# Output tiles that use two pools of accumulator banks in turn, and a small product that is placed later

## The chip, the core and the metric

The kernel runs on one core of a Trainium2 chip. A core has TensorE (PE, matrix products into PSUM, which has eight banks here), VectorE (DVE), ScalarE (ACT), GpSimd (POOL) and SyncE (SP, which issues the DMAs). Each engine works through its own instructions in order; between engines they wait on semaphores. The metric is the device time of one execution in microseconds, as the median of several runs.

## The reference

Two layers of a decoder trunk on x of shape (1, 512, 1024) in float32. Each layer is network 1, a token mixer, network 2, each behind an adaptive norm and added to x through a gate:

```python
mod = jax.nn.silu(c) @ w_mod[l] + b_mod[l]
sh1, sc1, g1, sh2, sc2, g2, sh3, sc3, g3 = jnp.split(mod[:, None, :], N_MOD, axis=-1)
h = _rmsnorm(x) * (1.0 + sc1) + sh1
x = x + HALF_STEP * g1 * _swiglu(h, ffn1_w_gate[l], ffn1_w_up[l], ffn1_w_down[l])
h = _rmsnorm(x) * (1.0 + sc2) + sh2
x = x + g2 * _hybrid_mixer(h, w_in[l], w_out[l], ...)
h = _rmsnorm(x) * (1.0 + sc3) + sh3
x = x + HALF_STEP * g3 * _swiglu(h, ffn2_w_gate[l], ffn2_w_up[l], ffn2_w_down[l])
```

`_swiglu` is (silu(h Wgate) * (h Wup)) Wdown, with 2816 hidden columns. The mixer joins stick-breaking attention, dilated attention and a gated recurrence, and projects back with w_out. The modulation `mod` is a product of one row with a 1024 x 9216 matrix for each layer.

## The kernel before, in words

Everything is kept transposed: x lives in SBUF as eight tiles X[0..7] (printed as x_84 to x_91), each 128 of the 1024 model columns by 512 tokens. Each float32 operand of a large product is split into a high and a low part (hi, lo), and a product is three matmuls (`triple`): hi*hi, hi*lo, lo*hi.

**Networks.** There are four (two in each layer). The 22 blocks of hidden columns are taken in three groups of 8, 8 and 6. In a group the gate and up products come first (PSUM tiles `m` and `a`; some pairs of blocks use a seven-product scheme, `seven`), then the down products: eight output tiles d = 0 to 7, each summed over the group's 8 (or 6) hidden blocks, so 24 (or 18) matmuls to a tile. The first two tiles of a group are made by `down_two` (it walks both tiles over the first n-2 blocks and then over the last two), the others by `down`. Each finished output tile is added to X[d] by one DVE instruction, `residual`, which multiplies by the gate and thereby empties the bank. In the last group of three of the four networks, tiles 2 to 7 are made in two halves of 256 tokens, so that the next norm (`norm`) can begin on the first half; then `first` starts the next stage's products with two `m` and two `a` banks.

**Banks.** PSUM is shared by two pools: `M` ("m", two banks) and `B` ("a", six banks). A tile is taken by `get`, which hands out the bank that is free the longest by the planner's account. In the kernel before, every output tile of a network takes an `m` bank.

**The modulation.** `background` runs through w_mod in pieces of 128 rows: DVE multiplies each piece by its value of silu(c) and adds it to `acc`; after eight pieces DVE reduces `acc` to 32 columns (`p`, an instruction that transposes and sums), PE sums over partitions with one small product (`a<-p,quads`), and DVE writes the result into `mod`. 16 such products are spread over the program.

**The order of the work.** The kernel is written as many generators ("streams"), which hand out steps. A planner (`Flow`, lines 229 to 356) runs them against its own account of when each engine and tile is ready, and always advances the step that can start first, with a bias by rank; what it emits is the fixed order of each engine's instructions. `Flow.start` (line 326) adds a margin to PE steps: MARGIN (0.65 us) for streams of rank 0, and LATE (line 66) for rank 4, which only `background` has. LATE is how long after its `p` the planner thinks ready it will place the small product at the earliest. Nearly all instructions are recorded by one helper, so the profile gives them line 116 (L116); tiles tell them apart.

Of the kernel before, what the change touches and what calls it, by code (L numbers as in the profile page):

```python
# [62 lines left out]
BR = -0.15  # L63
BA = (-0.1, -0.1)
BN = (-0.15, -0.1)
LATE = 2.0
LOP = ((1, 2, 3), (1, 2, 3, 4, 5, 6, 7))

SPANS = tuple((sum(GROUPS[:i]), n) for i, n in enumerate(GROUPS))
# [159 lines left out]
class Flow:  # L229
# [96 lines left out]
    def start(self, s):  # L326
# [6 lines left out]
        t = self.clk[st.engine] if st.engine != "SP" else self.clk["PE"]  # L333
        late = self.MARGIN if st.engine == "PE" and s[0] == 0 else LATE if st.engine == "PE" and s[0] == 4 else 0.0
        for a in st.deps:
# [24 lines left out]
def trunk(ctx, tc, x, c, w_mod, b_mod, f1g, f1u, f1d, w_in, w_out, qng, kng, hng, lbl, f2g, f2u, f2d, cf, out):  # L360
# [6 lines left out]
    def space(name, bufs, **kw):  # L367
        return ctx.enter_context(tc.tile_pool(name=name, bufs=bufs, **kw))
# [8 lines left out]
    M = Pool(F, space("psm", 2, space=PS), "m", [P, S], 2)  # L377
    B = Pool(F, space("psa", 6, space=PS), "a", [P, S], 6)
# [36 lines left out]
    def when(*keys):  # L415
        return lambda: all(k in done for k in keys)
# [526 lines left out]
    def part(w, k, i=None):  # L943

        o = slice(0, 256) if i is None else slice(i * P, (i + 1) * P)
        return tuple(z[:, k % 4, o] for z in w[k // 4])

    def triple(ps, wh, wl, xh, xl, start, stop, skip=False):
        T.matmul(ps, wh, xh, start=start, stop=False, skip_group_check=skip)
        T.matmul(ps, wh, xl, start=False, stop=False, skip_group_check=skip)  # L950
        T.matmul(ps, wl, xh, start=False, stop=stop, skip_group_check=skip)
# [184 lines left out]
    def residual(phase, d, ps, l, jg, cs):  # L1136
        if jg != 5 or not isinstance(phase, tuple):
            yield when(("mod", l, jg))
        yield Step("DVE", ps, bias=BR)
        V.scalar_tensor_tensor(X[d][:, cs], ps[:, cs], mod(l, jg, d), X[d][:, cs], ALU.mult, ALU.add)  # L1140
        drop(ps)
        for t in range(2):
            if cs.start <= t * HALF and cs.stop >= (t + 1) * HALF:
                done.add((phase, d, t))
# [32 lines left out]
    def ffn(phase, l, jsh, hs, last):  # L1177
# [3 lines left out]
        for f0, n in SPANS:  # L1181
# [58 lines left out]
            for f in range(f0, f0 + n, 2):  # L1240
# [15 lines left out]
                if f in fast:  # L1256
                    yield when((phase, "sums"))
                    for name, pools, fin in (("g", (M, M, B), gate_seven), ("u", (B, B, B), up_seven)):
                        w = yield from next_weight()
                        yield Step("PE", need=tuple((p, pools.count(p)) for p in (M, B) if p in pools))  # L1260
                        banks = [p.get() for p in pools]
# [6 lines left out]
                for pool, fin in ((M, gate_out), (B, up_out)):  # L1268
                    w = yield from next_weight()
                    for i in range(2):  # L1270
                        yield Step("PE", need=((pool, 1),))
                        ps = pool.get()
# [17 lines left out]

            def down(w, d, cs):
                yield when(keys[0])
                yield Step("PE", need=((M, 1),))
                ps = M.get()
                for k in range(n):
                    yield when(keys[k])
                    hi, lo = hid[k]
                    wh, wl = part(w, k, d % 2)
                    yield Step("PE", lo, wh, wl)
                    triple(ps[:, cs], wh, wl, hi[:, cs], lo[:, cs], k == 0, k == n - 1)  # L1300
                F.spawn(residual(key, d, ps, l, jg, cs), 0)

            def down_two(w, cuts):

                yield Step("PE", need=((M, 2),))
                banks = [M.get() for _ in range(2)]
                for ks in cuts:
                    for d, ps in enumerate(banks):
                        for k in ks:
                            yield when(keys[k])  # L1310
                            hi, lo = hid[k]
                            wh, wl = part(w, k, d)
                            yield Step("PE", lo, wh, wl)
                            triple(ps, wh, wl, hi, lo, k == 0, k == n - 1)
                        if ks[-1] == n - 1:
                            F.spawn(residual(key, d, ps, l, jg, FULL), 0)
# [4 lines left out]
            for d in range(0, whole, 2):  # L1321
                w = yield from next_weight()
                if d == 0:
                    yield from down_two(w, (range(n - 2), range(n - 2, n)))
                else:
                    for i in range(2):
                        yield from down(w, d + i, FULL)
                release(w)
            if whole < ND:
                ws = []  # L1330
                for t, cs in enumerate(HALVES):
                    for d in range(whole, ND):
                        if t == 0 and d % 2 == 0:
                            ws.append((yield from next_weight()))
                        w = ws[(d - whole) // 2]
                        yield from down(w, d, cs)
                        if t and d % 2:
                            release(w)
                WS.most -= MORE
# [649 lines left out]
```

## Time and profile before

| | |
|---|---|
| median of 3 runs | 2092.57 us (2092.12 to 2093.74) |
| the profiled execution's own time | 2094.81 us |
| its span, first to last instruction | 2092.4 us |
| PE busy in the span | 2050.3 us |
| DVE / ACT / POOL busy | 1586.0 / 1005.1 / 183.6 us |
| mean granted TensorE clock | 0.992 |
| matmul records | 12956 |

A row of the timeline has the start in us from the span's start, the time to the end of the last of the merged instructions, the engine, the line, the operation, the tiles (out<-in), the shape, the count, and in brackets the engine's idle time before it with what ended it. A matmul's recorded duration overlaps that of the next one, so merged rows overlap a little, and an idle gap of PE is counted from the end of the last matmul's record. Waits are listed as engine and tile, waited for engine and tile, total us, times, longest. Windows give each engine's busy time in a stretch of the span with its count of instructions, and the granted TensorE clock as a share of full speed.

### The profile page before, as it was taken

How to read it: one execution, taken by the hardware profiler on the slowest of the kernel's cores; microseconds unless marked ns; L12 is line 12 of the kernel's file. 1: busy time of each engine (PE TensorE's matmuls, PEld its weight loads, DVE VectorE, ACT ScalarE, POOL GpSimd, SP SyncE). 2: the span in 40 equal slices, each digit the busy share in tenths (PEclk: the TensorE clock that was granted, in tenths of full speed). 3: DMA queues.
4: the chain of work that ended last, by engine and by line, in shares of the span. 5: the costliest groups of instructions: out<-in, count | busy, mean ns of one | idle time of the engine just before them, and what ended most of it. 6: DMA issues, size and time to landing. Idle time of an engine off the chain costs nothing.

```text
span 2092.4 us, 32600 instructions
## 1 busy us (share of the span) xinstructions
PE 2050.3 (98%) x12956; PEld 1855.7 (89%) x12956; DVE 1586.0 (76%) x2510; ACT 1005.1 (48%) x1675; POOL 183.6 (9%) x224
## 2 busy tenths in 40 slices
PE   7999999999999999999999999999999999999999
PEld 6888889988888987999898899989888889889897
DVE  6887877686698776879686888867867978658584
ACT  5523434555855542544354253436476645325351
POOL 0000000150150100000010000012304200000000
PEclk8999999999999999999999999999999999999999
DMA  9376466211203245345524635643112141533321
GB/s 330 117 230 191 151 218 204 81 60 41 71 21 99 94 133 169 109 154 182 181 69 134 221 101 181 197 146 102 41 41 66 36 127 55 186 96 101 101 82 41
DMA packets 210569, 259.46 MB, mean 124 GB/s; under 512 B 8896, under 2 KB 192084, under 8 KB 210416
## 3 DMA queue, kind: packets, MB, share of 16 engines
q1 hardware_dynamic: 210160, 257.30, 38.5%
q8 instruction: 101, 1.65, 0.3%
q14 instruction: 52, 0.43, 0.1%
q0 software_dynamic: 256, 0.08, 0.0%
HBM read 255.25 MB, written 2.10 MB: 123 GB/s over the span
## 4 chain that ended last, share of the span: by engine, by line
PE 93%; DVE 4%; ACT 2%; issue 1%; DMA 1%; SPq 0%; DVEq 0%; ACTq 0%
PE m L116 56%; PE a L116 37%; ACT u L116 1%; DVE u L116 1%; DVE wt L116 1%; DVE x L116 1%; DVE h L116 1%; DVE acc L116 0%; ACT wt L116 0%; DMA w<-in_ffn_w_up_dram 0%; DMA u<-in_x_dram 0%; DVE k L116 0%; ACT L1471 0%; ACT L116 0%; SPq L116 0%
## 5 line engine op out<-in xcount | busy, mean ns | idle before, releaser
L116 ACT CAST wt<-w 128x1024 fp32r<-128x1024 f32 (+1 forms) x456 | 437.6, 975 | 328.4 <-PE m L116 124.0
L116 DVE TENSOR_TENSOR wt<-w,wt 128x1024 fp32r<-128x1024 f32 (+1 forms) x456 | 518.6, 1144 | 95.3 <-ACT wt L116 86.2
L116 PE MATMUL m<-u,wt 128*128 128x512 f32 (+1 forms) x2820 | 576.7, 362 | 6.3 <-DVE x L116 4.2
L116 PE MATMUL m<-h,wt 128*128 128x256 f32 (+1 forms) x2892 | 551.8, 342 | 11.6 <-ACT h L116 5.5
L116 PEld LDWEIGHTS m<-u,wt 128*128 128x128 f32 x2820 | 475.4, 190 | 85.7 <-DVE x L116 5.6
L116 PEld LDWEIGHTS m<-h,wt 128*128 128x128 f32 x2892 | 451.0, 192 | 69.4 <-ACT u L116 6.6
L116 PE MATMUL a<-h,wt 128*128 128x256 f32 (+1 forms) x2124 | 347.4, 318 | 0.0
L116 PEld LDWEIGHTS a<-h,wt 128*128 128x128 f32 x2124 | 308.3, 191 | 26.5
L116 DVE TENSOR_TENSOR u<-u 128x256 f32<-128x256 f32 (+4 forms) x444 | 255.3, 593 | 34.5 <-ACT u L116 30.7
L116 PE MATMUL a<-hs,wt 128*128 128x256 f32 x1944 | 250.8, 283 | 0.0
L116 POOL TENSOR_TENSOR u<-u 128x256 f32<-128x256 f32 x162 | 137.6, 869 | 1284.8 <-ACT u L116 1237.5
L116 PEld LDWEIGHTS a<-hs,wt 128*128 128x128 f32 x1944 | 241.0, 192 | 0.0
L116 DVE SCALAR_TENSOR_TENSOR x<-m,mod,x 128x512 f32<-128x512 f32 (+1 forms) x142 | 92.2, 651 | 111.7 <-PE m L116 111.0
L116 ACT ACTIVATE u<-u 128x512 f32<-128x512 f32 (+2 forms) x272 | 146.7, 567 | 49.2 <-POOL u L116 29.3
L116 DVE TENSOR_TENSOR w<-w 128x512 f32<-128x512 f32 x216 | 149.0, 690 | 6.2 <-DMA w<-in_ffn_w_gate_dram 0.6
L116 DVE SCALAR_TENSOR_TENSOR acc<-w,sc_c,acc 128x1024 f32<-128x1024 f32 x112 | 143.6, 1282 | 1.8
L116 PEld LDWEIGHTS a<-u 128*128 128x128 f32 x864 | 114.7, 191 | 11.8 <-issue 2.1
L116 ACT COPY u<-a 128x256 f32<-128x256 f32 (+1 forms) x149 | 58.1, 390 | 129.9 <-PE a L116 127.6
L116 PE MATMUL a<-u 128*128 128x64 f32 (+4 forms) x864 | 117.0, 282 | 1.9 <-DVE u L116 0.8
L116 ACT COPY u<-m 128x256 f32<-128x256 f32 (+1 forms) x119 | 49.7, 418 | 123.4 <-PE m L116 117.2
L116 ACT CAST u<-u 128x512 fp32r<-128x512 f32 (+1 forms) x96 | 58.4, 611 | 102.7 <-DVE u L116 93.4
L116 PE MATMUL m<-wt,h 128*128 128x256 f32 x768 | 99.7, 287 | 0.9 <-DVE u L116 0.9
(146 smaller groups left out, 1452.6 us busy)
## 6 DMA issues: line engine op xcount, KB each, us to landing
w<-in_w_mod_dram SPq DMA_DIRECT2D x128, 512.0 KB, 4.3
w<-in_ffn_w_gate_dram SPq DMA_DIRECT2D x88, 512.0 KB, 4.7
w<-in_ffn_w_up_dram SPq DMA_DIRECT2D x88, 512.0 KB, 4.9
w<-in_ffn_w_down_dram SPq DMA_DIRECT2D x80, 512.0 KB, 4.7
w<-in_w_in_dram SPq DMA_DIRECT2D x56, 512.0 KB, 3.8
u<-in_w_mod_dram SPq DMA_DIRECT2D x32, 256.0 KB, 6.0
w<-in_w_out_dram SPq DMA_DIRECT2D x24, 256.0 KB, 3.1
w<-in_ffn_w_down_dram SPq DMA_DIRECT2D x16, 256.0 KB, 5.7
```

The lines of the kernel that those rows point to most:

```text
L116: ins = fn(*args, **kw)
```

## The change

Two things change. The output tiles of a network take an `m` bank for even d and an `a` bank for odd d, in `down` and in `down_two`. And LATE grows from 2.0 to 5.0. No instruction is added or removed.

```diff
-LATE = 2.0
+LATE = 5.0
...
             def down(w, d, cs):
                 yield when(keys[0])
-                yield Step("PE", need=((M, 1),))
-                ps = M.get()
+                pool = (M, B)[d % 2]
+                yield Step("PE", need=((pool, 1),))
+                ps = pool.get()
...
             def down_two(w, cuts):
 
-                yield Step("PE", need=((M, 2),))
-                banks = [M.get() for _ in range(2)]
+                yield Step("PE", need=((M, 1), (B, 1)))
+                banks = [M.get(), B.get()]
```

Since the planner decides the order, the diff does not show what moves. Set beside each other, the two programs have PE's 12534 matmuls other than the 16 small products in the same order (only the norm's product over `ones` comes six matmuls later at three places); what differs there is the bank and where the small products stand. SP's and POOL's orders are the same; DVE's and ACT's are changed locally.

The first place is PE in network 2 of the first layer, the output tiles of the first group of hidden blocks (24 matmuls to a tile, the first two interleaved as 18, 18, 6, 6). Before:

```order
L116 MATMUL m<-u,wt 128x512 x42
L116 MATMUL a<-p,quads 128x32
L116 MATMUL m<-u,wt 128x512 x150
```

and now:

```order
L116 MATMUL m<-u,wt 128x512 x18
L116 MATMUL a<-u,wt 128x512 x18
L116 MATMUL m<-u,wt 128x512 x6
L116 MATMUL a<-u,wt 128x512 x6
L116 MATMUL m<-u,wt 128x512 x9
L116 MATMUL a<-p,quads 128x32
L116 MATMUL m<-u,wt 128x512 x15
L116 MATMUL a<-u,wt 128x512 x24
```

The tiles alternate between the pools, and the small product stands behind 57 of the matmuls instead of 42.

The second place is DVE at the same spot, from the small product's `p` on. Before:

```order
L116 TENSOR_REDUCE p<-acc 128x32
L116 SCALAR_TENSOR_TENSOR mod_92<-a,bcol_94 32x8 x4
L116 SCALAR_TENSOR_TENSOR x_84<-m,mod_92,x_84 128x512
L116 TENSOR_TENSOR wt<-w,wt 128x1024
L116 SCALAR_TENSOR_TENSOR x_85<-m,mod_92,x_85 128x512
```

and now:

```order
L116 TENSOR_REDUCE p<-acc 128x32
L116 TENSOR_TENSOR wt<-w,wt 128x1024 x2
L116 SCALAR_TENSOR_TENSOR mod_92<-a,bcol_94 32x8 x4
L116 SCALAR_TENSOR_TENSOR x_84<-m,mod_92,x_84 128x512
L116 SCALAR_TENSOR_TENSOR x_85<-a,mod_92,x_85 128x512
L116 SCALAR_TENSOR_TENSOR x_86<-m,mod_92,x_86 128x512
```

Two weight parts (`wt`, the low half of a weight) come ahead of the four instructions that read the small product; the additions to X (x_84 is tile 0) that empty the first banks come behind them.

The third place is PE where network 1 of the first layer ends and the mixer begins: the last group, two whole tiles, then tiles 2 to 7 in two halves, then the first products of the next stage from `h`. Before:

```order
L116 MATMUL m<-u,wt 128x512 x36
L116 MATMUL m<-u,wt 128x256 x129
L116 MATMUL a<-u,ones 128x256
L116 MATMUL m<-u,wt 128x256 x87
L116 MATMUL m<-h,wt 128x256 x24
L116 MATMUL a<-u,ones 128x256
L116 MATMUL m<-h,wt 128x256 x24
```

and now, from the end of the first product over `ones` on:

```order
L116 MATMUL a<-u,ones 128x256
L116 MATMUL a<-u,wt 128x256 x15
L116 MATMUL m<-u,wt 128x256 x18
L116 MATMUL a<-u,wt 128x256 x18
L116 MATMUL m<-u,wt 128x256 x18
L116 MATMUL a<-u,wt 128x256 x18
L116 MATMUL m<-h,wt 128x256 x30
L116 MATMUL a<-u,ones 128x256
L116 MATMUL m<-h,wt 128x256 x18
```

The last tile before the next stage (d = 7) is now in an `a` bank, and the one before it (d = 6) in an `m` bank, while the next stage starts with both `m` banks.

## Prediction

> **What bounds the kernel now.** I read the page's busy times first, then PE's waits, then the timeline of PE at each wait, then what DVE does there.
>
> ```profile
> PE 2050.3 (98%) x12956; PEld 1855.7 (89%) x12956; DVE 1586.0 (76%) x2510; ACT 1005.1 (48%) x1675; POOL 183.6 (9%) x224
> PE 93%; DVE 4%; ACT 2%; issue 1%; DMA 1%; SPq 0%; DVEq 0%; ACTq 0%
> ```
>
> PE is busy for 98% of the span and makes 93% of the chain that ended last. The change leaves PE's work as it is, so it can only win or lose in PE's waits and in the speed at which PE runs behind them. The waits of PE:
>
> ```profile
> PE m L116 <- DVE x L116: 7.5, 10, 2.0
> PE a L116 <- ACT u L116: 6.3, 10, 1.2
> PE m L116 <- ACT h L116: 5.5, 6, 1.7
> PE m L116 <- ACT u L116: 4.9, 6, 1.7
> PE a L116 <- DMA ident<-in_constants_dram: 3.2, 1, 3.2
> PE a L116 <- DVE p L116: 2.8, 1, 2.8
> ```
>
> The first row is PE waiting for an `m` bank that DVE has not emptied into X; the last is the small product waiting for its `p`. These are what the change can touch: 7.5 + 2.8 = 10.3 us, not all of it, but with what follows on each wait. No row names `wt`: PE never waits for a weight.
>
> For the price of a wait the undisturbed step is needed:
>
> ```profile
> L116 PE MATMUL m<-u,wt 128*128 128x512 f32 x2004 | 474.0, 394 | 3.8 <-DVE x L116 3.7
> L116 PE MATMUL m<-h,wt 128*128 128x256 f32 x1452 | 196.3, 288 | 9.5 <-ACT h L116 3.7 <-DVE x L116 3.3 <-ACT u L116 2.4
> 1815.68 10.14 PE L116 MATMUL m<-u,wt 128*128 128x512 f32 x44
> 688.27 3.04 PE L116 MATMUL m<-u,wt 128*128 128x256 f32 x24
> ```
>
> A 512-wide matmul is recorded with 0.394 us, and 44 of them take 10.14, so one follows the other after (10.14 - 0.394)/43 = 0.227. For 256 wide it is (3.04 - 0.288)/23 = 0.120. The rest of a record (0.167 in both cases) overlaps the next, so a gap of g in a row costs PE g + 0.17.
>
> **Part 1: the small product that waits** (network 2 of the first layer, first group's output tiles; PE, then DVE):
>
> ```profile
> 790.47 9.68 PE L116 MATMUL m<-u,wt 128*128 128x512 f32 x42
> 802.98 0.64 PE L116 MATMUL a<-p,quads 128*128 128x32 f32 x2 [2.83 <-DVE p L116]
> 803.43 8.77 PE L116 MATMUL m<-u,wt 128*128 128x512 f32 x26
> 801.68 1.25 DVE L116 TRANSPOSE_TENSOR_REDUCE p<-acc 128x32 f32<-128x1024 f32 x1
> ```
>
> Behind the gap the 26 matmuls take 8.77 where 0.394 + 25 x 0.227 = 6.07 is normal: 2.70 more. The cause is the granted clock, which stands at half in these windows:
>
> ```profile
> 798.00:802.00 4.00, 2.16 (x10) 1.46 (x8) 3.93 (x5) 0.53 (x1) 0.00 (x0) 1.00 0.60 185
> 802.00:805.00 3.00, 2.02 (x6) 1.73 (x7) 2.19 (x6) 0.00 (x0) 0.00 (x0) 0.52 0.95 313
> 1829.00:1832.00 3.00, 3.00 (x9) 2.37 (x9) 1.52 (x2) 0.03 (x1) 0.00 (x0) 0.59 1.10 349
> 1162.00:1170.00 8.00, 6.56 (x30) 5.46 (x31) 5.96 (x10) 2.40 (x3) 0.00 (x0) 1.00 0.65 197
> ```
>
> The small product itself also runs slow, 0.45 to the next start where the one at 1825.66 below has 0.14: 0.31. The site costs 2.83 + 0.17 + 0.31 + 2.70 = 6.0 us. In the changed order it stands behind 57 matmuls instead of 42. PE gets there at 790.47 + 57 x 0.227 = 803.4; `p` is done at 801.68 + 1.25 = 802.9, and the DVE instructions ahead of it are the same. So the wait goes, by a margin of only 0.5 us.
>
> **Part 2: output tiles that wait for a bank.** Tile 0 of a group ends after 42 matmuls and tile 2 begins after 48. With two `m` banks tile 2 needs the bank of tile 0, so DVE has 6 x 0.227 = 1.4 us to empty it. Twice it is late:
>
> ```profile
> 1150.90 11.04 PE L116 MATMUL m<-u,wt 128*128 128x512 f32 x48
> 1163.44 5.07 PE L116 MATMUL m<-u,wt 128*128 128x512 f32 x21 [1.50 <-DVE x L116]
> 1162.64 0.75 DVE L116 SCALAR_TENSOR_TENSOR x<-m,mod,x 128x512 f32<-128x512 f32 x1
> 1825.66 0.31 PE L116 MATMUL a<-p,quads 128*128 128x32 f32 x2
> 1825.80 0.94 PE L116 MATMUL m<-u,wt 128*128 128x512 f32 x3
> 1828.79 7.59 PE L116 MATMUL m<-u,wt 128*128 128x512 f32 x25 [2.04 <-DVE x L116]
> 1827.98 1.41 DVE L116 SCALAR_TENSOR_TENSOR x<-m,mod,x 128x512 f32<-128x512 f32 x2
> ```
>
> At 1163 the price is 1.50 + 0.17, and 5.07 - 0.394 - 20 x 0.227 = 0.14 behind it: 1.8 us, with the clock at 1.00 in its window above. At 1828 it is 2.04 + 0.17, and 7.59 - 0.394 - 24 x 0.227 = 1.75 at the lower clock: 4.0 us. With the change tile 2 takes the other `m` bank, and tile 4 is the first that needs tile 0's, after 96 matmuls, 48 x 0.227 = 10.9 us later than before. DVE's late instructions end at 1163.39 and about 1828.7 (the first of the two), so both waits go with about 10 us to spare. What is late next: in the changed order the addition of tile 0 near 802 stands behind two weight parts and `mod`.
>
> ```profile
> 805.95 1.99 ACT L116 CAST wt<-w 128x1024 fp32r<-128x1024 f32 x2 [7.42 <-PE m L116]
> L116 DVE TENSOR_TENSOR wt<-w,wt 128x1024 fp32r<-128x1024 f32 (+1 forms) x456 | 518.6, 1144 | 95.3 <-ACT wt L116 86.2
> 803.66 0.69 DVE L116 SCALAR_TENSOR_TENSOR mod<-a,bcol 32x8 f32<-32x8 f32 x4 [0.73 <-PE a L116]
> ```
>
> Their casts wait until PE has done 48 matmuls (790.47 + 10.9 + 0.17 = 801.5) and end at 803.5; 1.14 for the second part, 0.69 for `mod` and 0.75 for the addition make 806.1. Tile 4 comes at 790.47 + 96 x 0.227 = 812.3: 6 us to spare, and the same at 1826.
>
> **Part 3: from a network's split tiles into the next stage.** Three times (393, 1062, 1418) the pair of rows is the same; the first, and DVE beside it:
>
> ```profile
> 393.62 0.59 PE L116 MATMUL m<-h,wt 128*128 128x256 f32 x3 [0.17 <-ACT h L116]
> 394.71 2.78 PE L116 MATMUL m<-h,wt 128*128 128x256 f32 x21 [0.50 <-DVE x L116]
> 1063.98 2.77 PE L116 MATMUL m<-h,wt 128*128 128x256 f32 x21 [0.50 <-DVE x L116]
> 1419.66 2.77 PE L116 MATMUL m<-h,wt 128*128 128x256 f32 x21 [0.50 <-DVE x L116]
> 393.00 0.47 DVE L116 SCALAR_TENSOR_TENSOR x<-m,mod,x 128x256 f32<-128x256 f32 x1
> 394.19 0.47 DVE L116 SCALAR_TENSOR_TENSOR x<-m,mod,x 128x256 f32<-128x256 f32 x1
> 397.13 0.87 DVE L116 SCALAR_TENSOR_TENSOR h<-u,mod,h 128x256 fp32r<-128x256 f32 x2
> ```
>
> The next stage starts with both `m` banks, and needs the additions of tiles 6 and 7. The profile puts the first gap down to ACT, but it ends 0.15 us after the addition at 393.00 + 0.47, and the second 0.05 after the one at 394.19. I read both as bank waits: 0.17 + 0.17 + 0.50 + 0.17 = 1.0 us, three times: 3.0. Now tile 7 is in an `a` bank, so the stage needs tile 4's and, three matmuls later, tile 6's bank. Tile 6's addition ended at 393.47, and PE would now want it at 393.28 + 0.36 = 393.64: just met. The next limit is `h`: its last two low parts end at 398.0, and the eighth block of six matmuls begins at 393.28 + 7 x 0.72 = 398.3. So the 1.0 us holds, closely.
>
> **The other 14 small products and the cost of the alternation.** PE's row for `p` counts one wait, so the later place of the others wins nothing; PE does the same work for it. On DVE, which works in order, the four `mod` instructions wait for PE, up to 15 x 0.227 = 3.4 us longer each, and weight parts and additions stand behind them. DVE is idle for 24% of the span, and the weights are ahead of PE (no `wt` row among its waits), so I take nothing, with 0 and 3.4 us for each of 16 products as bounds. The change of pool from tile to tile is seen in the mixer's output projection:
>
> ```profile
> 678.92 0.87 PE L116 MATMUL a<-u,wt 128*128 128x256 f32 x6
> 679.63 0.88 PE L116 MATMUL m<-u,wt 128*128 128x256 f32 x6
> 680.35 0.88 PE L116 MATMUL a<-u,wt 128*128 128x256 f32 x6
> ```
>
> Six matmuls to 0.71 or 0.72 us is 0.12 each, as within one bank: the alternation is free. [...]
>
> **The sum.** 6.0 + 1.8 + 4.0 + 3.0 = 14.8 us. I take off 0.5 for the narrow margins of parts 1 and 3: 14.3. The profiled execution took 2094.81 us (span 2092.4, 2.4 around it); 2094.81 - 14.3 = 2080.5. The median of the runs shown is 2.24 us below the profiled one, so 2092.57 - 14.3 = **2078.3 us**.
>
> **Rivals.**
>
> A: the waits are replaced by the next ones. For: the margins of 0.5 us in part 1 and about none in part 3; PE waits elsewhere for ACT (6.3 + 5.5 + 4.9 us), and a PE that comes earlier may wait longer there. Against: DVE and ACT are mostly released by PE, so they come earlier with it. If part 3 gives nothing and the small product still waits for 1 us without a fall of the clock: 14.8 - 3.0 - 1.2 = 10.6, or 2082. If it waits long enough for the clock to fall, half of part 1 goes too: 2085.
>
> B: the clock falls elsewhere, or not because of these waits. Two falls of 2.70 and 1.75 us are in my sum. Gaps of 2.04 and 2.83 us were followed by half clock, one of 1.50 was not. If the falls stay or strike at other gaps, 14.8 - 4.8 = 10.0 is left: 2082.6. [...]
>
> C: the change doesn't do what it says, and the gain is lost to its own cost. `a` banks are also taken by the up products and the seven-product scheme behind each group; if these now wait 1.2 us (one addition of 0.75 and a little) at each of 12 group ends: 14.8 - 14.4, about 2092. Against: six `a` banks.
>
> D, slower: DVE stands at `mod`. In one product after the other DVE waits up to 3.4 us longer for PE, and the weight parts behind it come late. If it reaches PE for all 16: 16 x 3.4 = 54, less 14.8: 2132; it decides against me as soon as 5 of the 16 reach PE in full (17.0 against 14.8). Against it: no `wt` wait now, and at the place shown the new order puts two weight parts ahead of `mod`.
>
> **How the numbers follow.** Forecast (2075 to 2081): 0.74. A and B together (2081 to 2087): 0.17. C: 0.05. D: 0.04. Gaps are short and the clock's falls differ in length, so the forecast's own range is 3 us to each side; to leave out no more than 2 in 10 the range reaches into A and B: 2074.5 to 2085.5. About 0.2% (4.2 us) can be told from no change here, so below 2088.4 counts as faster: forecast, A and B: 0.91. Same: C: 0.05. Slower: 0.04.
>
> **What would show it.** In the changed profile the row of PE for DVE `p` is gone or below 0.5 us, that of `m` for DVE `x` falls from 7.5 to about 2.4 (what is left is in the mixer's output projection and the two starts behind it), the windows near 800 and 1820 have a clock of 1.00, and the gaps of 0.50 at the three network ends are gone. I am wrong if a PE row for `wt` or for an `a` bank appears, or if DVE rows show `mod` waiting for PE with PE idle behind it.

## The result and the profile after

The changed kernel takes 2077.41 us (median of 4 runs, 2076.63 to 2078.20) against 2092.94 us (4 runs, 2092.12 to 2093.74) before: a ratio of 0.993, 95% interval 0.9917 to 0.9942, or 15.5 us. The forecast was 2078.3. The profiled execution took 2076.63 us, its span is 2074.9. The busy times of its page and its chain that ended last:

```profile
PE 2040.7 (98%) x12956; PEld 1849.5 (89%) x12956; DVE 1586.0 (76%) x2510; ACT 1003.3 (48%) x1674; POOL 187.0 (9%) x224
PE 94%; DVE 2%; ACT 2%; DMA 1%; issue 0%; SPq 0%; ACTq 0%; DVEq 0%
```

PE has the same 12956 matmul records and is busy for 9.6 us less, much of it because fewer of them run at half clock (below; the mean granted clock is 0.994 against 0.992). PE's waits:

```profile
PE a L116 <- ACT u L116: 7.3, 10, 1.6
PE m L116 <- ACT h L116: 4.9, 3, 1.7
PE m L116 <- ACT u L116: 4.6, 5, 1.7
...
PE m L116 <- DVE x L116: 2.3, 4, 0.9
```

The row of `a` for DVE `p` (2.8 us) is gone, and `m` for DVE `x` fell from 7.5 to 2.3. No row for a weight has come. The timeline of PE at the four places of the sum, and of DVE at the first:

```profile
390.95 3.76 PE L116 MATMUL m<-h,wt 128*128 128x256 f32 x30
...
797.90 2.21 PE L116 MATMUL m<-u,wt 128*128 128x512 f32 x9
799.95 0.31 PE L116 MATMUL a<-p,quads 128*128 128x32 f32 x2
800.09 3.66 PE L116 MATMUL m<-u,wt 128*128 128x512 f32 x15
...
1151.01 5.60 PE L116 MATMUL m<-u,wt 128*128 128x512 f32 x24
...
1815.00 3.66 PE L116 MATMUL m<-u,wt 128*128 128x512 f32 x15
```

```profile
798.23 1.25 DVE L116 TRANSPOSE_TENSOR_REDUCE p<-acc 128x32 f32<-128x1024 f32 x1
799.40 2.32 DVE L116 TENSOR_TENSOR wt<-w,wt 128x1024 fp32r<-128x1024 f32 x2
801.63 0.68 DVE L116 SCALAR_TENSOR_TENSOR mod<-a,bcol 32x8 f32<-32x8 f32 x4
802.35 0.75 DVE L116 SCALAR_TENSOR_TENSOR x<-m,mod,x 128x512 f32<-128x512 f32 x1
```

`p` ends at 798.23 + 1.25 = 799.48, the product starts at 799.95: a margin of 0.47 us where 0.5 was forecast. The first addition, which needs that product's `mod`, ends at 803.1; tile 2 has been running since 797.90, in the other `m` bank. None of the rows has a gap in brackets, and the 15 matmuls behind the product take 3.66 = 0.394 + 14 x 0.233, nearly the undisturbed step of 0.227. The windows (PEclk is the last but two of a row) agree:

```profile
798.00:804.00 6.00, 6.00 (x29) 5.01 (x28) 5.86 (x11) 2.10 (x2) 0.00 (x0) 1.00 0.78 262
1813.00:1822.00 9.00, 9.00 (x42) 7.46 (x42) 3.60 (x9) 0.00 (x0) 0.00 (x0) 1.00 0.81 258
```

PE's large matmuls stand in the same order in both kernels, so each can be matched with itself, and the difference of its two start times shows where the kernel gained:

| place (us in the kernel before) | forecast | gained |
|---|---|---|
| small product near 802 | 6.0 | 5.9 |
| tile 2 at 1163 | 1.8 | 1.80 |
| tile 2 at 1828 | 4.0 | 3.97 |
| three network ends | 3.0 | 3.5 (1.16, 1.16, 1.15) |
| 994, an ACT wait of 0.37 that is now 0.02 | none | 0.36 |
| first 41 us | none | 2.2 |

Without the last row these are 15.5 us, the difference of the medians. The last row is no effect of the change: the code there is the same. Of its 2.2 us, 0.6 are other waits in the first 24 us, and the rest is how long PE ran at half clock in that one execution, here in the window 34 to 37 us of before, and then of after:

```profile
34.00:37.00 3.00, 3.00 (x9) 2.32 (x8) 2.71 (x5) 2.97 (x4) 0.00 (x0) 0.50 1.10 348
```

```profile
34.00:37.00 3.00, 3.00 (x14) 2.50 (x13) 2.89 (x5) 2.04 (x2) 0.00 (x0) 0.97 1.10 349
```

### The profile page after: what moved, and what is told of

The parts are those of the page before. It is cut to its first block, busy times and chain, and to the rows that moved or that the text cites. A ratio compares the mean times of both kernels' runs of the same rounds, so it can differ in the third digit from the quotient of the medians.

```text
span 2074.9 us, 32589 instructions
## 1 busy us (share of the span) xinstructions
PE 2040.7 (98%) x12956; PEld 1849.5 (89%) x12956; DVE 1586.0 (76%) x2510; ACT 1003.3 (48%) x1674; POOL 187.0 (9%) x224
## 4 chain that ended last, share of the span: by engine, by line
PE 94%; DVE 2%; ACT 2%; DMA 1%; issue 0%; SPq 0%; ACTq 0%; DVEq 0%
PE a L116 48%; PE m L116 46%; ACT u L116 1%; DMA w<-in_ffn_w_up_dram 1%; DVE u L116 1%; DMA u<-in_w_mod_dram 1%; DVE x L116 0%; ACT wt L116 0%; DVE wt L116 0%; SPq L116 0%; DVE acc L116 0%; DVE h L116 0%; DVE k L116 0%; ACT L1472 0%; ACT L116 0%
## 5 line engine op out<-in xcount | busy, mean ns | idle before, releaser
L116 PE MATMUL m<-u,wt 128*128 128x512 f32 (+1 forms) x1602 | 336.3, 359 | 2.8 <-ACT u L116 1.3
L116 PEld LDWEIGHTS m<-u,wt 128*128 128x128 f32 x1602 | 267.0, 189 | 45.7 <-ACT u L116 1.6
L116 PE MATMUL a<-u,wt 128*128 128x512 f32 (+1 forms) x1386 | 279.0, 353 | 0.0
L116 PEld LDWEIGHTS a<-u,wt 128*128 128x128 f32 x1386 | 229.4, 189 | 34.6
L116 DVE SCALAR_TENSOR_TENSOR x<-m,mod,x 128x512 f32<-128x512 f32 (+1 forms) x85 | 54.5, 642 | 76.9 <-PE m L116 76.2
```

The costliest lines, as they stand in the source:

```text
L116: ins = fn(*args, **kw)
```

## The experiments

Each diff is against the changed kernel. Times are medians, and each ratio is to runs of the kernel before on the same chip. The kernel before took 2092.3, 2091.5 and 2092.1 us on the chips of these experiments, against 2092.9 above, so a difference between the medians of two runs is sure only to about 1 us.

**The later product alone.** Is each half of the change worth its own part?

```diff
-                pool = (M, B)[d % 2]
-                yield Step("PE", need=((pool, 1),))
+                yield Step("PE", need=((M, 1),))
...
-                banks = [M.get(), B.get()]
+                banks = [M.get() for _ in range(2)]
```

> LATE 5.0 with every output tile still in an m bank. My theory now: the two parts are not independent, as the prediction had them. Three of the small products (the ones that make the gates of the network that is running: first group of network 1 and of network 2 in layer 1, and of network 2 in layer 2) are themselves ahead of the first addition to X, and with two m banks tile 2 waits for that addition. So the product cannot go behind 57 matmuls; in this kernel's order it stands behind 48 (and 45 in network 1), directly ahead of tile 2. PE then waits for p about 1.4 us near 802 and for the bank about 1.9 us right after (product to mod 0.7, addition 0.75 and hops), with the clock at half behind it; near 1826 the bank wait grows from 2.0 to about 2.7 us, and near 135 a new one of 1 to 2 us appears. Time 2093 to 2097 us, no gain. Rival (the parts are independent, as the prediction's sum had it): 6.0 less, 2087 us.

Measured: 2095.88 us, ratio 1.0018 (1.0008 to 1.0029). Alone, the later product is a small loss. Its waits, PE's timeline and two windows:

```profile
PE m L116 <- DVE x L116: 12.1, 11, 3.2
```

```profile
136.07 19.11 PE L116 MATMUL m<-u,wt 128*128 128x512 f32 x76 [2.04 <-DVE x L116]
...
805.06 0.41 PE L116 MATMUL a<-p,quads 128*128 128x32 f32 x2 [1.47 <-DVE p L116]
808.68 11.49 PE L116 MATMUL m<-u,wt 128*128 128x512 f32 x40 [3.22 <-DVE x L116]
...
1831.63 10.70 PE L116 MATMUL m<-u,wt 128*128 128x512 f32 x46 [1.57 <-DVE x L116]
```

```profile
806.00:813.00 7.00, 4.32 (x10) 3.48 (x11) 6.82 (x12) 1.04 (x1) 0.00 (x0) 0.53 0.58 177
1831.60:1836.00 4.40, 4.37 (x19) 3.67 (x20) 0.63 (x1) 0.00 (x0) 0.00 (x0) 1.00 1.11 353
```

The product near 802 makes the very gate by which DVE multiplies the first addition. With two `m` banks tile 2 (after 48 matmuls) cannot start before that addition, so the planner can place the product no later than there: it still waits for `p` (1.47), and the addition behind it then holds tile 2 for another 3.22. The same comes up at 136, where no wait was before. Only at 1831 was the wait shorter (1.57, with 2.7 expected) and no fall of the clock came behind it.

**The pools alone.**

```diff
-LATE = 5.0
+LATE = 2.0
```

> Both pools for the output tiles, LATE still 2.0. The small product near 802 stands behind 42 matmuls again. Theory: its wait of 2.8 us and the half clock behind it (2.7 us) stay, all bank waits go: 2077.4 + 5.9 = 2083.3 us. In the profile PE has a row for p of about 2.8 us, and m for DVE x is about 2.3 us. Rival (the pools do everything, and the product's wait was made by the bank waits or is taken up elsewhere): 2077 to 2079 us.

Measured: 2082.90 us, ratio 0.9959 (0.9946 to 0.9971), 0.4 us from what was expected.

```profile
800.99 0.41 PE L116 MATMUL a<-p,quads 128*128 128x32 f32 x2 [2.83 <-DVE p L116]
801.24 1.88 PE L116 MATMUL a<-u,wt 128*128 128x512 f32 x6
802.92 6.97 PE L116 MATMUL m<-u,wt 128*128 128x512 f32 x24
```

```profile
PE a L116 <- DVE p L116: 3.7, 2, 2.8
PE m L116 <- DVE x L116: 2.3, 4, 0.9
```

The wait of part 1 is there again with its 2.83 us, and slow matmuls behind it; parts 2 and 3 are gone. But the 30 matmuls behind the product take only 1.73 us longer here than the same counts in the changed kernel (1.88 for 6 where 1.52 is normal, and 6.97 for 24 where 5.60 is), about 3.5 us at half clock by estimate from these rows. In the profile before, 26 matmuls took 2.70 us longer, with a clock of 0.51 from 802 to 809. By the match of matmuls the site costs 4.7 us here and not 5.9. Another 1.1 comes from a second product, near 268, which waits 0.88 us here, but neither in the kernel before nor in the changed one. That the time fits the expectation so well is in part luck. So by the medians the pools are worth about 10 us alone, and the later product another 5.5 us, but only on top of them: -10.0 and +2.9 alone do not add up to -15.5.

**Which tiles need the pools.** First the two first tiles in both pools and the rest in `m`, then the two first in `m` and the rest in both.

```diff
# first two only
-                pool = (M, B)[d % 2]
-                yield Step("PE", need=((pool, 1),))
-                ps = pool.get()
+                yield Step("PE", need=((M, 1),))
+                ps = M.get()
# rest only
-                yield Step("PE", need=((M, 1), (B, 1)))
-                banks = [M.get(), B.get()]
+                yield Step("PE", need=((M, 2),))
+                banks = [M.get() for _ in range(2)]
```

> LATE 5.0; only the pair of tiles 0 and 1 takes an m and an a bank, tiles 2 to 7 take m banks as before. Theory: what counts within a group is that tile 2 finds a bank, so the waits near 802, 1163 and 1828 stay away; the last two tiles of a network are both in m banks again, so the waits of 0.17 and 0.50 us at the three network ends come back: 2077.4 + 3.5 = 2080.9 us. Rival (the alternation as such is what helps): most of the gain is gone, above 2085 us.

Measured: 2081.09 us, ratio 0.9950 (0.9937 to 0.9962).

```profile
PE m L116 <- DVE x L116: 3.8, 7, 0.9
```

> LATE 5.0; tiles 0 and 1 both in m banks as before, tiles 2 to 7 in m and a in turn. Theory: tile 2 waits for tile 0's bank as in the kernel before, and the product stands at 48 as in the kernel with LATE alone; only the network ends are helped (3.5 us): about 3.5 us below the kernel with LATE alone, 2089 to 2094 us. Rival (alternation as such): 2080 us or less.

Measured: 2091.72 us, ratio 0.9998 (0.9989 to 1.0007).

```profile
PE m L116 <- DVE x L116: 10.6, 8, 3.2
```

Both came as expected. One bank moved in each group (tile 1) brings 10 to 12 of the 15.5 us: it frees the `m` bank that tile 2 takes, and with it the place for the later product. The alternation of tiles 2 to 7 brings what is left, the network ends (seven waits against four).

**The product at 3.0 instead of 5.0.** Is 5.0 just enough?

```diff
-LATE = 5.0
+LATE = 3.0
```

> The changed kernel with LATE 3.0 instead of 5.0. The small product near 800 then stands behind 48 matmuls instead of 57; p was done in the changed kernel at 799.48, PE is there at about 797.9: a gap of about 1.4 us, no bank wait behind it. Theory (a wait of this length costs itself and 0.17 us, and does not lower the clock, as the one of 1.50 us at 1163 did not): 2077.4 + 1.6 = 2079.0 us. Rival (any wait in this place brings half clock for 3.4 us, as the wait of 2.8 us did): 2080.7 to 2082.4 us.

Measured: 2087.72 us, ratio 0.9982 (0.9974 to 0.9991). Both expectations missed, though the place they spoke of did as the first said: a gap of 1.47 us and a clock of 1.00 behind it, 1.8 us in all by the match of matmuls.

```profile
802.51 0.41 PE L116 MATMUL a<-p,quads 128*128 128x32 f32 x2 [1.47 <-DVE p L116]
```

```profile
803.00:808.00 5.00, 5.00 (x23) 4.09 (x23) 4.89 (x10) 1.06 (x1) 0.00 (x0) 1.00 0.53 176
```

Of the other 8.5 us, 6.6 were lost in the mixers, far from any product that waits: 2.6 us between 430 and 495 of the changed kernel and 4.0 between 1440 and 1512, by the match of matmuls (within these stretches the orders differ, at their ends they agree again). Another 1.5 went near 1640; its cause is not shown. The changed kernel has two gaps of 1.18 and 0.44 us there and a clock of 1.00 from 1636 to 1644. A new wait appears:

```profile
PE m L116 <- DVE k L116: 4.5, 2, 2.3
```

DVE in this kernel, and then in the changed one:

```profile
478.72 0.75 DVE L116 SCALAR_TENSOR_TENSOR u<-u,par 128x512 f32<-128x512 f32 x1 [3.93 <-ACT u L116]
...
485.09 1.39 DVE L116 TENSOR_TENSOR k<-m,k 64x512 fp32r<-64x512 f32 x2
```

```profile
481.62 1.39 DVE L116 TENSOR_TENSOR k<-m,k 64x512 fp32r<-64x512 f32 x2 [1.06 <-ACT k L116]
```

The two instructions that empty an `m` bank there stand behind other work on DVE in this kernel. One constant moved a few products, and the planner put a different order into a stage that has nothing to do with them.

**The product at 4.5**, for the margin at 802.

```diff
-LATE = 5.0
+LATE = 4.5
```

> The changed kernel with the product placed at 4.5 instead of 5.0: at 802 it stands 3 matmuls (0.68 us) earlier, so the margin of 0.47 us there becomes a gap of 0.2 us (0.2 + 0.17 on the clock). Theory (only a gap long enough lowers the clock, the price is the gap): 2077.8, with PE's row a<-DVE p at 0.2 us and clock 1.00 behind it. Rival (the planner's order elsewhere decides, as at 3.0, where the mixer's k rows came late for 7 us): PE's row for DVE k appears again and the time is 2081-2088.

Measured: 2078.70 us, ratio 0.9939 (0.9927 to 0.9952).

```profile
800.56 0.41 PE L116 MATMUL a<-p,quads 128*128 128x32 f32 x2
```

The gap is 0.1 us for 0.2 expected (the row ahead ends at 798.93 + 1.52 = 800.45), the matmuls there are 0.39 us later than in the changed kernel, no row for `k` came, and nothing else moved by more than 0.2 us behind the opening. So the margin of 0.47 us was real: with 0.68 us less, PE waits.

**The product at 8.0.** Does the slower rival, DVE standing at `mod`, exist at all?

```diff
-LATE = 5.0
+LATE = 8.0
```

> The changed kernel with LATE 8.0. The small products go later again (behind 69 matmuls near 800). Theory (once the product is not waited for, its place does not matter; DVE's longer stand at mod is hidden): 2077.4 us, within 0.8. Rival (DVE's stand at mod, up to 3 us longer for each product, makes the weight parts and additions behind it late): above 2080 us, with PE rows for DVE wt or more for DVE x.

Measured: 2127.57 us, ratio 1.0172 (1.0159 to 1.0185). PE now waits for weights:

```profile
PE m L116 <- ACT wt L116: 20.4, 4, 8.8
PE m L116 <- DVE wt L116: 15.4, 4, 6.4
```

By the match of matmuls, in the changed kernel's time, 13.9 us went at 407 to 427 (start of the first mixer), 12.6 at 1074 to 1085, 4.0 at 1113 to 1122, 6.1 at 1369 to 1381 and 14.5 at 1425 to 1435. At the first of these, PE, DVE and ACT of this kernel, and then ACT and DVE of the changed one:

```profile
419.23 4.84 ACT L116 CAST wt<-w 128x1024 fp32r<-128x1024 f32 x5
420.33 1.23 PE L116 MATMUL m<-h,wt 128*128 128x512 f32 x2 [4.56 <-ACT wt L116]
421.50 5.22 DVE L116 SCALAR_TENSOR_TENSOR acc<-w,sc_c,acc 128x1024 f32<-128x1024 f32 x4
```

```profile
403.08 1.03 ACT L116 CAST wt<-w 128x1024 fp32r<-128x1024 f32 x1
420.29 1.26 DVE L116 SCALAR_TENSOR_TENSOR acc<-w,sc_c,acc 128x1024 f32<-128x1024 f32 x1
```

Here the casts of the mixer's first weights come only at 419, behind other work in ACT's order, and four pieces of the modulation (`acc`), each in a slot for raw rows, are still to be worked off at 421; the changed kernel makes one of the casts at 403 already and works off one piece at 420. DVE does not stand at `mod` here. I took it that the raw slots are filled by modulation rows that nothing may use yet. That can be tried: more slots.

```diff
-RAW = (8, 4)
+RAW = (10, 4)
```

> The changed kernel with the small product placed at 8.0 (as in the run that took 2127.6 us) and the number of slots for raw weight rows raised from 8 to 10 outside the mixers. Theory: later products hold back the additions into acc, the modulation's raw rows (2 slots each) stay in the slots that the weights need, and the casts for the mixer's first weights come too late; with 2 more slots these waits shrink: PE's rows for ACT wt and DVE wt, 20.4 + 15.4 us at slots 8, fall below 15 together, and the time falls by at least 15 us, to 2085-2112. Rival: DVE and ACT are late at the mixer's start for another reason (DVE stands at mod, or the order of the gates); then the wt waits stay within 5 us of 35.8 and the time at 2122-2132. The same slots with the product at 5.0, beside it, tell what the slots do by themselves.

Measured: 2098.06 us, ratio 1.0031 (1.0019 to 1.0044).

```profile
PE m L116 <- DVE wt L116: 9.3, 2, 8.7
PE m L116 <- ACT wt L116: 4.5, 1, 4.5
```

> The changed kernel with 10 instead of 8 slots for raw rows, product at 5.0. It is the control of the run before: the slots alone. PE has no wait for a weight in the changed kernel, so more raw rows ahead win nothing: 2077-2080 by the theory that raw slots matter only where modulation rows fill them; a loss by up to 10 us where the planner's other order makes other waits (two runs so far lost 10 us so); a gain of more than 2 us would say that weights were short in the changed kernel too.

Measured: 2081.34 us, ratio 0.9951 (0.9936 to 0.9966). The slots alone cost 3.9 us, more than the theory had; by the match of matmuls 3.2 of it went near 427, where PE waits 1.53 us for a weight part and 1.04 for ACT. At 8.0 the slots win 29.5 us. The waits for weights fall from 35.8 to 13.8 us, and the losses at 1074 to 1085, 1113 to 1122, 1369 to 1381 and 1425 to 1435 are won back (12.6, 4.0, 6.1 and 14.5 us). The first mixer's start is not (16.1 us lost there against the changed kernel). So two more slots win back most of the loss at 8.0. They also give the planner another order of DVE's and ACT's work, and these runs do not tell the two apart; what holds the first start was not found.

**More of the same: the mixer's output projection.** Its first six tiles still take two `m` banks.

```diff
-            yield Step("PE", need=((M, 2),))
-            banks = [M.get() for _ in range(2)]
+            yield Step("PE", need=((M, 1), (B, 1)))
+            banks = [M.get(), B.get()]
```

> The changed kernel with the same alternation for the first six output tiles of the mixer's output projection (both banks there were m). Theory (the same mechanism): the two gaps of 0.15 and 0.25 us per layer that DVE x still causes there go, 0.32 + 0.42 twice: 2077.4 - 1.5 = 2075.9 us. Rival: the planner also reorders the end of attention here, and other waits take their place: 2077 to 2080 us.

Measured: 2087.73 us (2082.64 to 2091.78), ratio 0.9980 (0.9971 to 0.9990): worse than both expectations.

```profile
674.17 2.25 PE L116 MATMUL a<-u 128*128 128x512 f32 x11 [3.12 <-DVE u L116]
...
678.40 1.48 PE L116 MATMUL a<-u,wt 128*128 128x256 f32 x6
```

The free banks let the planner place matmuls of the projection earlier, between the last steps of the attention; near its end PE then has nothing left to lay over DVE's part. It waits 3.12 us, and then six matmuls take 1.48 where 0.88 is normal, three times in a row up to 682.

**The last half tiles in `a`**, once with the edit before and once alone.

```diff
-                pool = (M, B)[n % 2]
+                pool = B if t and n >= 2 else (M, B)[n % 2]
```

> As the kernel with the alternation in the output projection, and the last six half tiles of the mixer's output projection all take an a bank, so that network 2 finds both m banks free. PE's gaps there are 1.61 and 0.90 us in each layer, with 3.4 us of half clock behind them. Theory: DVE is busy without a break there (5.50 of 5.50 us in the kernel before, 701 to 706.5), and makes additions and the first h in turn, so PE waits for h instead of a bank: the gain is below 1 us in each layer, 2074 to 2076 us. Rival (they are bank waits like those of the change): 2 x (1.61 + 0.17 + 0.90 + 0.17 + 1.7) = 9 us less, 2067 us.

Measured together with the edit before: 2090.58 us, ratio 0.9995 (0.9986 to 1.0004). Both expectations missed: the loss of that edit is carried along, so the time says nothing on this one. By the match of matmuls its two places lose 1.7 and 1.3 us against the changed kernel. Alone:

> The changed kernel, and the last six half tiles of the mixer's output projection (after the first two of the second half) all take a banks instead of m and a in turn; the order of all instructions stays. In the changed kernel PE stands there at 697.09 and 698.58 for 1.61 + 0.90 us. If these are waits for the m banks alone, they vanish with their fall of the clock: 2 x (1.61 + 0.17 + 0.90 + 0.17 + 1.7) = 9.1 us, 2068. If the h rows that DVE makes are as late, new waits for h take their place, as in the run that had this edit together with the output tiles' alternation (0.60 + 1.42 + 0.28 us there, at half clock, the stretch 698-718 net 1.7 us longer and its twin 1.3): 2076.4 (0.5 us won at each place, clock as before) to 2080.4.

Measured: 2081.49 us, ratio 0.9951 (0.9939 to 0.9964), 4 us worse than the changed kernel. The place in the changed kernel, timeline and window:

```profile
697.09 0.59 PE L116 MATMUL m<-h,wt 128*128 128x256 f32 x3 [1.61 <-ACT h L116]
698.58 6.41 PE L116 MATMUL m<-h,wt 128*128 128x256 f32 x39 [0.90 <-DVE x L116]
```

```profile
699.50:703.00 3.50, 3.50 (x20) 3.50 (x19) 3.50 (x6) 2.05 (x4) 2.67 (x2) 0.54 0.10 29
```

And here:

```profile
700.59 0.98 PE L116 MATMUL m<-h,wt 128*128 128x256 f32 x6 [0.60 <-DVE h L116]
702.99 0.98 PE L116 MATMUL m<-h,wt 128*128 128x256 f32 x6 [1.42 <-DVE h L116]
```

```profile
1719.00:1726.00 7.00, 6.58 (x27) 5.89 (x28) 5.97 (x10) 4.62 (x9) 1.85 (x2) 0.54 0.00 1
```

The bank waits are gone, and 4 us later PE waits for `h`, which DVE makes no faster. The two gaps shown are 0.5 us shorter than the two before, but other short ones follow (up to 0.9 us, for `h` and for POOL), and from 1719 to 1726 the clock is 0.54, where the changed kernel has 0.57 from 1713 to 1717 at this place and 1.00 from 1718 to 1724. By the match of matmuls the two places lose 1.4 and 1.9 us, the opening 1.2. No version that was run is faster than the changed kernel.

## Why the prediction was right

**Part 1, the small product (6.0 forecast, 5.9 gained).** Gap, slow product and half clock went together, and the margin was 0.47 us for a forecast of 0.5. (Of the four windows shown for the half clock, the two at 802 and 1829 have it, with 0.52 and 0.59; the other two are at 1.00.) With the product 3 matmuls earlier there is a wait, which shows how close the place is. What the working did not say: the place after 57 matmuls exists only because tile 2 has another bank. The prediction counted parts 1 and 2 as if each could be had alone. Their sum was not touched by this, since both were made, but whoever had taken only the later product on the word of part 1 would have got a loss of 2.9 us instead of a gain of 6.0.

**Part 2, tile 2 (1.8 and 4.0 forecast, 1.80 and 3.97 gained).** Right in place and cause.

**How far the sizes show anything.** The forecast's terms and the gains in the table are read from the same profiled execution of the kernel before. Their agreement shows that these waits and what followed on them went, not what they cost in other executions. The half clock (2.70 and 1.75 of the 14.8) is what varies: behind the same gap of 2.83 us the matmuls took 2.70 us longer in the kernel before and 1.73 with the pools alone. That the medians differ by the table's 15.5 to a tenth is luck to that extent.

**Part 3, the network ends (1.0 each forecast, 1.16 gained).** The reading that both gaps are bank waits holds, though the profile put the first down to ACT: with the bank free there is no gap, and the 30 matmuls from 390.95 run through. `h`, named as the next limit, came just in time. The 0.16 more is what the sum left out here and counted in part 2, the slower rows behind the gaps: 3 matmuls in 0.59 us where the step of 0.120 gives 0.53, and 21 in 2.78 where it gives 2.69.

**No cost of the alternation.** Right: 24 matmuls of a tile take 5.60 = 0.394 + 23 x 0.226 in either pool, and no new PE row for an `a` bank appears.

**The 0.5 us taken off** for narrow margins did not come: nothing was lost at them. The sum before it, 14.8, is nearer to the 15.5 measured than 14.3. What it lacks is the 0.5 at the three network ends and the 0.36 at 994, which was not foreseen. That wait goes with the later product: it is gone with the product at 4.5 and with the later product alone, and there again at 3.0 and at 2.0.

**The rivals.** A's three pieces did not come in the changed kernel: `h` stayed just in time at the network ends, and behind the opening PE's waits for ACT are the same as before but for those that went at the network ends and at 994. It became the limit at the next place where two bank waits were taken away, the start of network 2. B: the clock followed the gaps, and when they went the falls went (1.00 from 798 to 804 and from 1813 to 1822). C did not come. D was put down to DVE standing at `mod`, with 3.4 us a product. DVE's wait there, before and after:

```profile
DVE mod L116 <- PE a L116: 25.4, 12, 3.4
```

```profile
DVE mod L116 <- PE a L116: 26.5, 11, 6.8
```

The longest is 3.4 us longer, as D said, but the sum grew by 1.1 us only, and no weight was late. At 8.0 weights are late and the kernel loses 35 us against the one before, but DVE's wait at `mod` is 28.7 us in all there, only 2.2 more than in the changed kernel: most of the loss comes by way of the raw slots and the planner's order, not by D's own mechanism.

## What to carry to other kernels

Price a wait with what follows on it: of the 15.5 us, the gaps themselves were about 11 and half clock behind two of them about 4.4, in one execution of the kernel before. The second part differs from one execution to the next (2.70 us behind the gap of 2.83 there, 1.73 behind the same gap with the pools alone). Before placing work later, ask which bank its result sets free: a place in the order that depends on a free bank has no value of its own, and one bank moved brought most of this gain. Where a planner makes the order, a small constant is an edit to the whole program; compare waits over the whole trace, since 3.0 and 8.0 in place of 5.0 lost 10 and 50 us, most of it in stages that the constant doesn't name.

## What the runs showed of the hardware

**Half clock came behind some gaps of PE and not behind others.** In the kernel before, a gap of 2.83 us (up to 802.98) was followed by a clock of 0.51 from 802 to 809, and one of 2.04 (up to 1828.79) by 0.59 from 1829 to 1832; gaps of 1.50 (up to 1163.44) and 1.70 (up to 1934.36) were not: 1.00 from 1162 to 1170 and from 1933 to 1937. In the changed kernel, 1.61 with 0.90 near 697 was followed by 0.54 over 3.5 us. In the runs, a gap of 1.57 (1831, later product alone) and gaps of 1.47 and 2.27 (802 and 486, product at 3.0) kept 1.00 in their windows, while 1.47 with 3.22 soon after (805 and 808, later product alone) gave 0.53 over 7 us. The same gaps need not be followed by the same clock: with the last half tiles in `a` alone, 0.60 with 1.42 came before 0.54 over 7 us from 1719 and before 0.76 over 7 us from 703.

**The length of a gap does not settle it.** Here 2.27 us kept the clock and 2.04 did not. What else decides was not shown. So the price of half clock behind a gap stands for the execution it was read from: behind 2.83 us it was 2.70 us in the kernel before and 1.73 with the pools alone.
